# Values and seven heads' gates by seven products of quarters in a stage ahead of the heads, with token sums in SBUF, and two products of the output projection sharing a quarter of the weight

## The chip, the cores and the metric

The kernel runs on one core of one Trainium2 chip. The time is device microseconds (us) of one execution, as the median of several runs. The profile is of one such execution. The engines are TensorE (PE, matmuls; PEld are its weight loads), VectorE (DVE), ScalarE (ACT), GpSimd (POOL) and SyncE (SP, which issues most transfers here). Tensors lie in DRAM, in SBUF (128 partitions) or in PSUM, where the PE writes its sums. "128x1024" is a tile of 128 partitions with 1024 elements each.

## The reference

The function is a backbone of two layers over 256 latent tokens and 256 context tokens, in float32, with a width D of 2048. Each layer normalises its input, scales and shifts it by vectors computed from a condition (`mod = silu(c) @ ada_w + ada_b`, one for latents, one for context), runs a mixer with a SiLU gate, and adds the gated result. Layer 0 is retention with 8 heads (queries and keys 256 wide, values and gates 512 wide each); layer 1 is attention. Cut to what the change touches:

```python
def project(h):                                   # h: tokens x 2048
    p = h @ w_in                                  # w_in: 2048 x 12288
    q = heads(p[..., :2048], 8, 256) * 256 ** -0.5
    k = heads(p[..., 2048:4096], 8, 256)
    v = heads(p[..., 4096:8192], 8, 512)
    g = p[..., 8192:]                             # 8 heads x 512
...
o = retention of (q, k, v), both directions       # decays 2 ** (lg2 * distance)
on = o * rsqrt(mean(o * o) + EPS) * norm_gain
y = (on * silu(g)) @ w_out                        # 4096 x 2048
x = x + gate_latent * y_latent; ctx = ctx + gate_context * y_context
```

## The kernel before, in words

**Split precision.** Each float32 operand is held as a high part (rounded, `fp32r` in the profile) and a low part (the rest). A product is three matmuls, high·high, high·low and low·high (`mm3`, lines 140 to 142); in later stages the low part of the tokens and the high part share one 512-wide matmul, and the third is 256 wide (lines 188 and 191, 986 and 989). A weight tile `wraw` is 128x1024, 512 KB; SP loads it (`load_raw`, three buffers), ACT casts the high part `wh` (line 132), DVE subtracts to get the low part `wl` (`sub`, line 113), and 24 matmuls of 512 columns use the pair.

**Stages.** (1) Normalisation, the first modulation vectors, and the queries and keys of heads 0 and 1. (2) The heads: for each head a product for the gate, one for queries and keys and one for the values (`gemm_ws`, `gemm_ts`), each of eight weight tiles. Between the tiles a `hook` runs: one step of `sum_jobs`, two steps of `ada_jobs`, and one task of the list `tasks` (`pump`), which holds the work of the head before: scores, outputs, norm, `spill` and `parts`. (3) The output projection by seven products of quarters, M1 to M7 (a scheme of Strassen's kind: sums and differences of quarters of the tokens and of the weight are multiplied, so that eight products become seven). (4) Layer 1: keys, values, gates, queries, attention, its output projection.

**Side work in the heads stage.** `ada_jobs` computes the remaining modulation vectors on DVE: it loads rows of `adaB` into `abraw` tiles (128x512), and a SCALAR_TENSOR_TENSOR with an accumulated sum (line 711) multiplies each with the condition's row `crow`, once for each of two conditions, and writes the product to `ajunk`. `sum_jobs` makes four of the projection's weight sums in DRAM (`wS_d`): ACT's queue copies one quarter there and POOL's queue adds another with an accumulating transfer; a one-column copy `pin_t` on POOL sets when it is issued. `decays` makes the table `dd` of a head with a power on POOL (line 776). `output` adds squares `ossq` on POOL (line 829) and multiplies by the gate `sg` on DVE (line 825), `parts` makes sums `ue` of quarters of the gated output, which go to `uB_d` in DRAM, on POOL (line 843). What one of these engines does is in the order in which the program issues it; a transfer starts when its buffer is free.

**M3 and M6** run one after the other: M3 with a quarter of `wo0`, M6 with `wS_d[1]`, each as `single`, which splits one tile for each step.

## Time and profile before

| what | value |
|---|---|
| time, median of three runs | 1963.08 us (1960.08 to 1963.69) |
| span of the profiled execution | 1959.6 us |
| instructions in the profile | 26859 |
| ACT cast `wh`, each | 1052 ns, 415 of them |
| bytes moved | 436.23 MB, mean 223 GB/s |
| PEclk | 9 tenths or more in every slice |

The profiled execution's own time is not given apart; its span is 3.5 us below the median of the runs. The profile divides the span in 40 equal slices of 49 us; a digit is the busy share of an engine in tenths. Slices 3 to 24 are the heads, to slice 32 the projection, the rest is layer 1. A row of a timeline has the start, the duration, engine, line, operation and tiles; "xN" gathers N neighbours, and a start-to-start distance is the cost of one in a busy queue, since neighbours overlap at their ends. A row of a group has the count, the busy time, the mean of one in ns, and behind the second bar the idle time before these instructions and what ended it.

### The profile page before, as it was taken

How to read it: one execution, taken by the hardware profiler on the slowest of the kernel's cores; microseconds unless marked ns; L12 is line 12 of the kernel's file. 1: busy time of each engine (PE TensorE's matmuls, PEld its weight loads, DVE VectorE, ACT ScalarE, POOL GpSimd, SP SyncE). 2: the span in 40 equal slices, each digit the busy share in tenths (PEclk: the TensorE clock that was granted, in tenths of full speed). 3: DMA queues.
4: the chain of work that ended last, by engine and by line, in shares of the span. 5: the costliest groups of instructions: out<-in, count | busy, mean ns of one | idle time of the engine just before them, and what ended most of it. 6: DMA issues, size and time to landing. Idle time of an engine off the chain costs nothing.

```text
span 1959.6 us, 26859 instructions
## 1 busy us (share of the span) xinstructions
PE 1945.1 (99%) x9612; PEld 1612.6 (82%) x9612; DVE 1350.5 (69%) x2518; ACT 752.2 (38%) x1126; POOL 481.6 (25%) x389
## 2 busy tenths in 40 slices
PE   8999999999999999999999999999999999999999
PEld 4678888888888888888888888888888888888887
DVE  5566223788888888888565645877879746777764
ACT  4234223132222232232232334455555434766653
POOL 1218635525525526526300301100000100000000
PEclk9999999999999999999999999999999999999999
DMA  9965668898898998998755445677876324433365
GB/s 392 410 221 165 195 179 232 253 317 253 261 309 251 268 309 242 275 301 242 231 190 198 145 136 174 223 242 269 276 244 216 109 90 162 146 135 139 130 204 172
DMA packets 152039, 436.23 MB, mean 223 GB/s; under 512 B 18240, under 2 KB 37024, under 8 KB 146272
## 3 DMA queue, kind: packets, MB, share of 16 engines
q1 hardware_dynamic: 118976, 346.88, 50.6%
q0 software_dynamic: 10640, 34.87, 10.0%
q10 hardware_dynamic: 22288, 52.75, 7.8%
q8 instruction: 75, 1.23, 0.2%
q14 instruction: 60, 0.49, 0.1%
HBM read 416.04 MB, written 85.51 MB: 256 GB/s over the span
## 4 chain that ended last, share of the span: by engine, by line
PE 97%; DMA 1%; DVE 1%; issue 0%; ACT 0%; SPq 0%; DVEq 0%; ACTq 0%
PE acc L140 19%; PE acc L141 19%; PE acc L142 19%; PE acc L989 9%; PE acc L191 6%; PE acc L986 5%; PE acc L188 3%; PE pm L140 3%; PE pm L141 3%; PE pm L142 3%; PE acc L513 2%; PE pm L989 2%; PE pm L450 1%; PE pm L986 1%; PE pm L1307 1%; DMA rows<-gamT_d 1%
## 5 line engine op out<-in xcount | busy, mean ns | idle before, releaser
L132 ACT CAST wh<-wraw 128x1024 fp32r<-128x1024 f32 x415 | 435.2, 1052 | 848.5 <-PE acc L141 305.7
L113 DVE TENSOR_TENSOR wl<-wraw,wh 128x1024 fp32r<-128x1024 f32 x416 | 512.1, 1235 | 338.1 <-ACT wh L132 303.8
L140 PE MATMUL acc<-hT_h,wh 128*128 128x512 f32 x928 | 363.2, 391 | 1.0 <-DVE r_l L113 1.0
L141 PE MATMUL acc<-hl,wh 128*128 128x512 f32 x928 | 361.4, 389 | 0.0
L142 PE MATMUL acc<-hT_h,wl 128*128 128x512 f32 x928 | 361.2, 389 | 0.0
L711 DVE SCALAR_TENSOR_TENSOR ajunk<-abraw,crow 128x512 bf16<-128x512 f32 x448 | 344.2, 768 | 21.0 <-DMA abraw<-in_adaB 11.7
L142 PE MATMUL acc<-wh,hl 128*128 128x512 f32 x704 | 274.4, 390 | 0.0
L140 PE MATMUL acc<-wh,hT_h 128*128 128x512 f32 x576 | 224.7, 390 | 0.0
L141 PE MATMUL acc<-wl,hT_h 128*128 128x512 f32 x576 | 224.4, 390 | 0.0
L140 PEld LDWEIGHTS acc<-hT_h,wh 128*128 128x128 f32 x928 | 174.3, 188 | 38.0 <-DVE r_l L113 1.4
L142 PEld LDWEIGHTS acc<-hT_h,wl 128*128 128x128 f32 x928 | 174.2, 188 | 36.4
L141 PEld LDWEIGHTS acc<-hl,wh 128*128 128x128 f32 x928 | 174.4, 188 | 34.8
L241 POOL TENSOR_TENSOR rs<-ms,mhalf 128x4 f32<-128x4 f32 (+1 forms) x23 | 32.7, 1420 | 605.1 <-DVE ms L238 303.1
L776 POOL TENSOR_TENSOR dd<-two,dd 128x128 f32<-128x128 f32 x8 | 168.5, 21064 | 19.1 <-DVE dd L774 19.1
L142 PEld LDWEIGHTS acc<-wh,hl 128*128 128x128 f32 x704 | 132.2, 188 | 27.5
L322 POOL COPY pin_t<-wl 128x1 f32<-128x1 f32 x128 | 64.1, 500 | 317.5 <-DVE wl L113 313.2
L140 PEld LDWEIGHTS acc<-wh,hT_h 128*128 128x128 f32 x576 | 108.2, 188 | 23.1 <-issue 1.1
L141 PEld LDWEIGHTS acc<-wl,hT_h 128*128 128x128 f32 x576 | 108.2, 188 | 21.7
L324 POOL DMA_DIRECT2D wS_d<-in_wo x128 | 109.6, 872 | 11.2 <-issue 10.0
L843 POOL TENSOR_TENSOR ue<-sg 128x512 f32<-128x512 f32 x38 | 66.8, 1770 | 100.5 <-DVE sg L833 40.2
L829 POOL TENSOR_TENSOR ossq<-ossq,osq 128x512 f32<-128x512 f32 x24 | 35.3, 1470 | 185.7 <-ACT osq L823 185.0
L140 PE MATMUL acc<-wh,hl 128*128 128x512 f32 x192 | 75.4, 393 | 0.0
(282 smaller groups left out, 2915.1 us busy)
## 6 DMA issues: line engine op xcount, KB each, us to landing
wraw<-in_w SPq DMA_DIRECT2D x272, 512.0 KB, 4.2
abraw<-in_adaB SPq DMA_DIRECT2D x256, 256.0 KB, 5.5
wraw<-in_wo SPq DMA_DIRECT2D x80, 512.0 KB, 4.2
wS_d<-in_wo ACTq DMA_DIRECT2D x128, 256.0 KB, 5.2
wS_d<-in_wo POOLq DMA_DIRECT2D x128, 256.0 KB, 6.7
wraw<-wS_d SPq DMA_DIRECT2D x64, 512.0 KB, 4.5
araw<-in_adaS SPq DMA_DIRECT2D x28, 1024.0 KB, 11.5
wraw<-uB_d SPq DMA_DIRECT2D x20, 512.0 KB, 4.4
```

Source lines behind the costliest of these rows:

```text
L113: return nc.vector.tensor_tensor(out=out, in0=a, in1=hi.bitcast(F32), op=ALU.subtract)
L132: last_hi[0] = nc.scalar.copy(wh, raw).ins
L140: nc.tensor.matmul(ps, lhsT=ah, rhs=bh, start=start, stop=False, skip_group_check=skip)
L141: nc.tensor.matmul(ps, lhsT=ah, rhs=bl, start=False, stop=False, skip_group_check=skip)
L142: return nc.tensor.matmul(ps, lhsT=al, rhs=bh, start=False, stop=stop, skip_group_check=skip).ins
L191: nc.tensor.matmul(accs[j], lhsT=wk, rhs=h1(kb, s).rearrange("p a t -> p (a t)"), start=(kb == 0), stop=False)
L324: nc.gpsimd.dma_start(out=wS_d[i, r, q, x], in_=wo0_d[(*SUMS[i][1], r, q, x)], accum_op=ALU.add, max_dma_last_dim=4096)
L711: nc.vector.scalar_tensor_tensor(out=junk, in0=raw, scalar=1.0, in1=crow[:, t, q * 512:(q + 1) * 512], op0=ALU.mult, op1=ALU.mult, accum_o ...
L776: nc.gpsimd.tensor_tensor(out=dd, in0=two.to_broadcast([P, P]), in1=dd, op=ALU.pow)
L843: (nc.vector if now else nc.gpsimd).tensor_tensor(out=ue, in0=x, in1=y, op=op)
L986: last_pe[0] = nc.tensor.matmul(accs[j][:, 0:L], lhsT=wk, rhs=b[:, 0:L], start=False, stop=(kq == 3 and k == 3)).ins
L989: nc.tensor.matmul(accs[j], lhsT=wk, rhs=b, start=(kq == 0 and k == 0), stop=False)
```

## The change

Line numbers move: the subtraction of line 113 is line 114 after, that of a general sum or difference (`comb`) line 117, the ada operation of line 711 line 684, 829 and 843 are 1060 and 1074.

- **A new stage ahead of the heads.** The queries and keys of heads 0 to 2 go to DRAM (`stash`, `qk_d`). In the product of head 2's, `stat_jobs` makes four sums of quarters of the tokens and splits them into the SBUF tiles `S` (16 sums on DVE, 16 on POOL, 128x512 each). Then come four units for the values, each of two heads, and seven for the gates of heads 0 to 6. A unit is seven products of quarters: 28 steps for a pair of values, 14 for a gate. Step i loads its raw tile, forms the weight's sum or difference for step i-1 (`form`, 128x1024, on POOL but for half of `Y2`), splits that of step i-2 and multiplies that of i-3. `join` adds products on DVE from PSUM and an SBUF tile, and results go to `v_d` and `g_d` in DRAM; a gate's halves are added on POOL first.
- **Side work there.** After each step but those of the third product an ada step runs in two of three, and a sum job in one of four.
- **The ada operations** are 1024 wide, one for each condition, half as many. Their raw tiles are `wraw` tiles, of which there are now five. The last of their four parts moves to layer 1, where every second hook has one.
- **The heads** have six hooks each: five products for queries and keys and one for a gate are left, and the tasks stand in `slots` at numbered hooks. Queries and keys, values and gates come from DRAM. `dd` is read from a table in DRAM.
- **M3 and M6** are one stage. POOL adds the first quarter to the second for M6, and the sum jobs make three sums instead of four.

In instructions: matmuls of 512 columns 7275 to 6187, of 256 columns 1696 to 3152; casts of `wh` on ACT 416 to 506; POOL operations on two tiles of 128x1024 none to 121; ada operations on DVE 448 of 128x512 to 224 of 128x1024.

On POOL in the heads stage, before: at the end of a head the sums of squares and the `ue` of `parts`, 512 columns wide, with the copies and transfers of the weight sums.

```order
L829 TENSOR_TENSOR ossq<-ossq,osq 128x512 x2
L241 TENSOR_TENSOR rs<-ms,mhalf 128x4
L322 COPY pin_t<-wl 128x1
L324 DMA wS_d<-in_wo 64x1024
L843 TENSOR_TENSOR ue<-sg 128x512 x2
```

After, on POOL in a unit of values (lines 760, 762, 764 and 767 are `form`; `vt` is the formed tile):

```order
L760 TENSOR_TENSOR vt<-wraw 128x1024 x2
L326 COPY pin_t<-wl 128x1
L328 DMA wS_d<-in_wo 64x1024
L760 TENSOR_TENSOR vt<-wraw 128x1024 x2
L326 COPY pin_t<-wl 128x1
L328 DMA wS_d<-in_wo 64x1024
L762 TENSOR_TENSOR vt<-wraw,vt 128x1024 x3
```

POOL has a two-tile operation of 1024 columns at every second step; before, its two-tile operations were 512 wide and eight of them came with a head. On POOL in a unit of gates, after (line 862 adds the halves of a result):

```order
L862 TENSOR_TENSOR f<-f 128x2x256
L760 TENSOR_TENSOR vt<-wraw 128x1024
L862 TENSOR_TENSOR e<-e 128x2x256
L760 TENSOR_TENSOR vt<-wraw 128x1024
L326 COPY pin_t<-wl 128x1
L328 DMA wS_d<-in_wo 64x1024
L862 TENSOR_TENSOR f<-f 128x2x256
L762 TENSOR_TENSOR vt<-wraw,vt 128x1024
```

There the adds of results stand between the forms. On DVE in the heads stage, before: one low half and four ada operations for each weight tile.

```order
L113 TENSOR_TENSOR wl<-wraw,wh 128x1024
L711 SCALAR_TENSOR_TENSOR ajunk,asum<-abraw,crow 128x512 x4
L833 SCALAR_TENSOR_TENSOR sg<-sg,vec,pm 128x512 x4
L113 TENSOR_TENSOR wl<-wraw,wh 128x1024
L711 SCALAR_TENSOR_TENSOR ajunk,asum<-abraw,crow 128x512 x4
```

After, on DVE in a unit of values: a low half at each step, for 12 matmuls, an ada operation at two of three, and the joins (`q_1766` is a partial result).

```order
L114 TENSOR_TENSOR wl<-wraw,wh 128x1024
L684 SCALAR_TENSOR_TENSOR wraw,asum<-wraw,crow 128x1024
L114 TENSOR_TENSOR wl<-vt,wh 128x1024
L114 TENSOR_TENSOR wl<-wraw,wh 128x1024
L684 SCALAR_TENSOR_TENSOR ajunk,asum<-wraw,crow 128x1024
L117 TENSOR_TENSOR q_1766<-pm,q_1766 128x512
L114 TENSOR_TENSOR wl<-vt,wh 128x1024
L117 TENSOR_TENSOR q_1766<-pm,q_1766 128x512
L684 SCALAR_TENSOR_TENSOR wraw,asum<-wraw,crow 128x1024
```

The low halves come twice as often for a matmul as before. The diff, cut to its core:

```diff
-ADAN = (2, 2, 2)
+ORDER4 = ("X0 Z0 X1 Z1 X2 Z2 X3 Z3", "Y0 Z0 Y1 Z1 Y2 Z2 Z3 Y3", "Y0 Y1 Y2 Y3", "X0 Y0 X1 Y1 X2 Y2 X3 Y3")
+ORDER2 = ("X0 Z0 X1 Z1", "Y0 Z0 Z1 Y1", "Y0 Y1", "X0 Y0 X1 Y1")
...
     def load_raw(src):
-        t = strm.tile([P, 2, 512], F32, name="wraw", tag="wraw", bufs=3)
+        t = strm.tile([P, 2, 512], F32, name="wraw", tag="wraw", bufs=5)
...
     def sum_jobs():
-        todo = [(i, r, q, slice(64 * x, 64 * x + 64)) for i in (2, 3, 0, 1) for r in range(4) for q in range(4)
+        todo = [(i, r, q, slice(64 * x, 64 * x + 64)) for i in (2, 3, 0) for r in range(4) for q in range(4)
...
+                for kb in range(KB):
+                    raw = load_raw(adaB_d[16 * part + kb, q].rearrange("p (a c) -> p a c", a=2))
+                    for t in range(ntk):
+                        flat = raw.rearrange("p a c -> p (a c)")
+                        junk = pool.tile([P, 1024], BF16, name="ajunk", tag="ajunk") if t < ntk - 1 else flat
+                        nc.vector.scalar_tensor_tensor(
+                            out=junk, in0=flat, scalar=1.0, in1=crow[t],
+                            op0=ALU.mult, op1=ALU.mult, accum_out=asum[:, q, kb, t:t + 1])
+                        if (kb, t) != (KB - 1, ntk - 1):
+                            yield
+                if q:
...
+        def stat_jobs():
...
+
+            for kp in range(4):
+                ra, rb = t2(0), t2(1)
+                r = [ra[:, 0], ra[:, 1], rb[:, 0], rb[:, 1]]
+                for j, x in enumerate(r):
+                    k, c = 2 * kp + 8 * (j % 2), half(j // 2)
+                    nc.vector.tensor_tensor(out=x, in0=hT_h[:, k:k + 2, c].bitcast(F32),
+                                            in1=hl[k // 2][:, :, c].bitcast(F32), op=ALU.add)
+                a11, a12, a21, a22 = r
+                for out, x, y, op in ((a22, a21, a22, ALU.add), (a21, a11, a21, ALU.subtract),
+                                      (a11, a22, a11, ALU.subtract), (a12, a12, a11, ALU.subtract)):
+                    nc.gpsimd.tensor_tensor(out=out, in0=x, in1=y, op=op)
+                yield
+                ks = slice(2 * kp, 2 * kp + 2)
+                for i, x in enumerate((a22, a11, a21, a12)):
+                    split(S[i][:, ks, 0, :], S[i][:, ks, 1, :], x)
+                yield
+
...
+            def load(self, g, m, kp):
+                for b in {"X0": (11,), "Z0": (11, 12), "Y1": (22,), "Z1": (22,), "Y2": (11,), "X3": (21,),
+                          "Y3": (21,)}[f"{m}{g}"]:
+                    if (g, b, kp) not in self.raws:
+                        self.raws[g, b, kp] = load_raw(self.piece(b, kp))
+
+            def form(self, g, m, kp):
+                raws, vt = self.raws, self.vt
+                pool = nc.gpsimd.tensor_tensor
+                if (g, m) == (0, "Z"):
+                    vt[kp] = ph.tile([P, 2, 512], F32, name="vt", tag=f"T{kp if self.n == 4 else kp + 2 * (self.h % 2)}")
+                    pool(out=vt[kp], in0=raws[0, 12, kp], in1=raws[0, 11, kp], op=ALU.subtract)
+                elif (g, m) == (1, "Y"):
+                    pool(out=vt[kp], in0=raws[1, 22, kp], in1=vt[kp], op=ALU.subtract)
+                elif (g, m) == (2, "Y"):
+                    (pool if kp % 2 else nc.vector.tensor_tensor)(
+                        out=raws[2, 11, kp], in0=vt[kp], in1=raws[2, 11, kp], op=ALU.subtract)
+                elif (g, m) == (3, "Y"):
+                    pool(out=vt[kp], in0=raws[3, 21, kp], in1=vt[kp], op=ALU.subtract)
+
+            def parted(self, g, m, kp):
+                src = {"X0": 11, "Z1": 22, "X3": 21, "Y2": 11}.get(f"{m}{g}")
+                self.sp[g, m, kp] = split_w(self.raws[g, src, kp] if src else self.vt[kp])
...
+                else:
+                    wh, wl = (x.rearrange("p a (k c) -> p (a k) c", k=2) for x in (wh, wl))
+                    for t in range(2):
+                        ts = slice(t * P, t * P + P)
+                        for k4 in range(4):
+                            first, end = new and (kp, k4) == (0, 0), last and k4 == 3
+                            mh, ml = op(4 * kp + k4)
+                            if i is not None:
+                                nc.tensor.matmul(acc[t], lhsT=wh[:, k4, ts],
+                                                 rhs=S[i][:, 4 * kp + k4].rearrange("p a t -> p (a t)"),
+                                                 start=first, stop=end, skip_group_check=True)
+                            else:
+                                nc.tensor.matmul(acc[t][:, 0:L], lhsT=wh[:, k4, ts], rhs=mh, start=first, stop=False,
+                                                 skip_group_check=True)
+                                nc.tensor.matmul(acc[t][:, L:T], lhsT=wh[:, k4, ts], rhs=ml, start=False, stop=end,
+                                                 skip_group_check=True)
+                        for k4 in range(4):
+                            mh, ml = op(4 * kp + k4)
+                            nc.tensor.matmul(acc[t][:, 0:L], lhsT=wl[:, k4, ts], rhs=mh, start=False,
...
+                wide_hook(g)
+                if last:
+                    self.join(g, m)
...
+            def join(self, g, m):
...
+                if (g, m) == (0, "X"):
+                    self.q1 = self.tile("q1")
+                    each(lambda t, a: nc.scalar.copy(self.q1[:, t], a))
+                elif (g, m) == (0, "Z"):
+                    self.e = self.tile("e")
...
+                    each(lambda t, a: comb(self.f[:, t], a, self.q1[:, t], ALU.add))
+                elif (g, m) == (1, "Y"):
+                    each(lambda t, a: comb(self.f[:, t], a, self.f[:, t], ALU.add))
+                    self.store(0, 1, self.f)
+                elif (g, m) == (3, "X"):
+                    x = self.tile("f")
...
+            def store(self, i, j, t):
+                def finish():
+                    if self.kind == "v":
+                        nc.scalar.dma_start(out=v_d[self.h + j, :, 2 * i:2 * i + 2], in_=t)
+                    else:
+                        nc.scalar.activation(t[:, :, 0:L], t[:, :, 0:L], AF.Silu)
+                        nc.scalar.dma_start(out=g_d[self.h, :, 2 * j:2 * j + 2, half(i)], in_=t[:, :, 0:L])
+
+                if self.kind == "g":
+                    nc.gpsimd.tensor_tensor(out=t[:, :, 0:L], in0=t[:, :, 0:L], in1=t[:, :, L:T], op=ALU.add)
+                later.append((step_n[0] + (3 if self.kind == "g" else 1), finish))
+
+        def wide_hook(g):
+            step_n[0] += 1
+            n = step_n[0]
+            if g != 2 and n % 3:
+                ada_step()
+            if n % 4 == 0:
+                next(sums, None)
+            while later and later[0][0] <= n:
+                with tc.issue_after(last_hi[0]):
+                    later.pop(0)[1]()
+
...
+        def hook():
+            with tc.issue_after(last_lo[0]), tc.issue_after(last_hi[0]):
+                next(stats, None)
+            ada_step()
...
+        stash(2, gemm_ws(w0_d, 6, 8, h_mov, T, hook=hook))
+        us = [Unit("v", h) for h in (0, 2, 4, 6)] + [Unit("g", h) for h in range(H - 1)]
+        steps = [(u, g, x[0], int(x[1])) for u in us for g, xs in enumerate(ORDER4 if u.n == 4 else ORDER2)
+                 for x in xs.split()]
+        for i in range(len(steps) + 3):
+            for what, back in (("load", 0), ("form", 1), ("parted", 2), ("mm", 3)):
+                if 0 <= i - back < len(steps):
+                    u, *a = steps[i - back]
+                    getattr(u, what)(*a)
+        for _, f in later:
+            f()
...
-            nc.gpsimd.tensor_tensor(out=dd, in0=two.to_broadcast([P, P]), in1=dd, op=ALU.pow)
+            nc.scalar.dma_start(out=dd, in_=skew_d[h, 127:127 + P * 254].rearrange("(p x) -> p x", x=254)[:, 0:P])
             return rows, dd
...
+                    (nc.scalar if h == H - 1 else nc.gpsimd).dma_start(out=uB_d[m, h], in_=ue)
             for m, x in ((M2, a), (M5, d)):
...
+                at(b + 1 - i, lambda h=h, i=i: v_load(h, i))
+            for i in range(4):
+                at(b + (0 if late else 2 + i // 2), lambda h=h, i=i: scores(h, 0, (2, 3, 0, 1)[i], *rd[h]))
...
+        def hook():
+            next_slot()
+            n = state["n"]
+            next(sums, None)
+            ada_step(2 if n % 4 else 1)
...
+        def weights36(r, kq):
+            a, b = quarter(wo0_d[0, 0], r, kq), quarter(wo0_d[1, 0], r, kq)
+            yield split_w(a)
+            nc.gpsimd.tensor_tensor(out=b, in0=b, in1=a, op=ALU.add)
+            yield split_w(b)
...
+    def hook1():
+        pump(PUMP)
+        ada1_n[0] += 1
+        if ada1_n[0] % 2:
+            ada1_hook()
```

More of the change, by code (lines that the diff above doesn't have):

```diff
@@ L739, in qk_evac, with grid, v_load @@
+        def grid(x):
+            return x.rearrange("p (r c) -> p r c", r=4)
+        def v_load(h, i):
+            raw = load_raw(v_d[h, :, 2 * i:2 * i + 2])
+            for t in range(2):
+                split(slot_h(4 + 2 * i + t)[:, :], slot_l(4 + 2 * i + t)[:, :], raw[:, t])
+        state = {"n": 0}
         def qk_evac(ps, i, base):
@@ L1034, in stage @@
                     hook(r, kq)
+                    next(sums, None)
         def single(m, src, done, hook):
@@ L1342, in backbone @@
                     attend(c, t)
+        for _ in ada1:
+            pass
         for g in range(4):
```

417 lines of the change are left out of this document (252 added, 165 removed).

## The prediction

> **What bounds the kernel now.** I read the page first: busy time, slices, chain.
>
> ```profile
> PE 1945.1 (99%) x9612; PEld 1612.6 (82%) x9612; DVE 1350.5 (69%) x2518; ACT 752.2 (38%) x1126; POOL 481.6 (25%) x389
> PE   8999999999999999999999999999999999999999
> ...
> DVE  5566223788888888888565645877879746777764
> ...
> POOL 1218635525525526526300301100000100000000
> PE 97%; DMA 1%; DVE 1%; issue 0%; ACT 0%; SPq 0%; DVEq 0%; ACTq 0%
> ```
>
> TensorE is busy 99% of the span and is 97% of the chain: a matmul removed is time removed, as long as VectorE (DVE), which makes the low half `wl` of every weight tile, keeps up. DVE runs at 8 tenths in the heads stage (slices 8 to 18). So I looked at one head (heads are periodic; 400 to 544.9 us is one), at the products M3 and M6 (1405 to 1493 us) and at layer 1, by a table of stretches (busy time and count of PE, weight loads, DVE, ACT, POOL, then clock, DMA share, GB/s), and at DVE's groups in that head:
>
> ```profile
> 400.00:544.90 144.90, 144.90 (x662) 120.48 (x661) 122.44 (x277) 39.91 (x57) 66.39 (x58) 1.00 0.90 279
> 1405.00:1493.00 88.00, 88.00 (x508) 77.29 (x507) 70.96 (x111) 47.12 (x72) 1.49 (x1) 1.00 0.72 244
> 1640.00:1880.00 240.00, 239.99 (x1265) 202.76 (x1264) 183.59 (x320) 153.93 (x266) 9.29 (x8) 1.00 0.43 145
> L711 DVE SCALAR_TENSOR_TENSOR ajunk<-abraw,crow 128x512 bf16<-128x512 f32 x99 | 74.8, 756 | 5.9 <-DMA abraw<-in_adaB 3.7
> L113 DVE TENSOR_TENSOR wl<-wraw,wh 128x1024 fp32r<-128x1024 f32 x24 | 30.4, 1266 | 7.9 <-ACT wh L132 3.6 <-POOL pin_t L322 2.0 <-DMA wraw<-in_w 1.4
> ```
>
> DVE is at 122.44 of 144.90 us; less `ajunk` and `wl`, some 17.5 us of it are the head's own work. The granted clock is 1.00, and transfers run to 279 GB/s with the PE still full.
>
> **Price of a matmul.** From the timeline of PE, starts of single ones in the heads, and of runs of eight near the end:
>
> ```profile
> 376.10 0.39 PE L141 MATMUL acc<-hl,wh 128*128 128x512 f32 x1
> 376.33 0.39 PE L142 MATMUL acc<-hT_h,wl 128*128 128x512 f32 x1
> ...
> 1902.12 2.00 PE L191 MATMUL acc<-hT_h,wh 128*128 128x512 f32 x8
> 1903.96 1.11 PE L188 MATMUL acc<-hT_h,wl 128*128 128x256 f32 x8
> 1904.92 0.86 PE L191 MATMUL acc<-hT_h,wh 128*128 128x512 f32 x3
> ```
>
> (1903.96−1902.12)/8 = 0.230 us for 512 columns, (1904.92−1903.96)/8 = 0.120 for 256.
>
> **Price of POOL beside DVE.** The change gives POOL operations on two SBUF tiles, 1024 wide. The widest of before are 512 wide (`ue`, `ossq`). The timelines of DVE and POOL around two pairs of them:
>
> ```profile
> 374.60 1.22 DVE L113 TENSOR_TENSOR wl<-wraw,wh 128x1024 fp32r<-128x1024 f32 x1
> 375.74 1.78 DVE L711 SCALAR_TENSOR_TENSOR ajunk<-abraw,crow 128x512 bf16<-128x512 f32 x1
> ...
> 379.26 0.69 DVE L711 SCALAR_TENSOR_TENSOR ajunk<-abraw,crow 128x512 bf16<-128x512 f32 x1
> ...
> 380.00 0.69 DVE L711 SCALAR_TENSOR_TENSOR ajunk<-abraw,crow 128x512 bf16<-128x512 f32 x1
> ...
> 380.62 2.34 DVE L113 TENSOR_TENSOR wl<-wraw,wh 128x1024 fp32r<-128x1024 f32 x1
> 374.78 3.89 POOL L843 TENSOR_TENSOR ue<-sg 128x512 f32<-128x512 f32 x2 [5.32 <-DVE sg L833]
> 380.58 3.52 POOL L843 TENSOR_TENSOR ue<-sg 128x512 f32<-128x512 f32 x2 [0.61 <-DMA uB_d<-ue]
> 358.93 0.69 DVE L825 TENSOR_TENSOR sg<-pm,sg 128x512 f32<-128x512 f32 x1
> 359.54 1.42 DVE L711 SCALAR_TENSOR_TENSOR ajunk<-abraw,crow 128x512 bf16<-128x512 f32 x1
> 358.84 3.25 POOL L829 TENSOR_TENSOR ossq<-ossq,osq 128x512 f32<-128x512 f32 x2
> L829 POOL TENSOR_TENSOR ossq<-ossq,osq x24: 1280/1537/1717, 255.2 to 1186.8; 128x512 f32<-128x512 f32 x24
> L1365 POOL TENSOR_TENSOR xo<-xo,half x12: 732/738/745, 1887.4 to 1935.8; 128x256 f32<-128x256 f32 x12
> ```
>
> The same `ajunk` takes 0.69 us alone and 1.78 beside POOL, `wl` 1.22 and 2.34: +1.09 and +1.12, with one POOL operation in each. The two engines go one after the other. `sg<-pm,sg`, one of whose inputs is in PSUM, keeps its 0.69 in the middle of POOL's `ossq`. So a POOL operation of 512 columns takes about 1.06 us (these two and a shorter one) from a DVE that reads two SBUF tiles, of its own shortest 1.280. From 738 ns (256 columns) to 1280 (512) POOL needs 542 per 256, so 1024 columns take 1.280+2×0.542 = 2.36 us; less the same 0.22 that did not hold DVE, 2.14. That is my price of a hold. The bounds: 1.06 if a hold doesn't grow with width, 2×1.28 = 2.56 if two whole short ones.
>
> The Trainium skill (SBUF — State Buffer, "Who interferes with whom") states that a DVE instruction with two SBUF inputs contends with a GpSimd one that reads SBUF, and that the first to issue keeps the shared ports for the whole instruction. The rows above agree at 512 columns; no row shows 1024. By that rule the hold is the 2.14 and the sum below +63; by the nearest row alone, 1.06, it is −42.
>
> DVE, start to start: `wl` 375.74−374.60 = 1.14; `ajunk` 0.74 and 0.62 (379.26, 380.00, 380.62), mean 0.68 with its accumulator read; a 512-wide operation of 0.69 about 0.61. For the 1024-wide `ajunk`:
>
> ```profile
> L113 DVE TENSOR_TENSOR wl<-wraw,wh 128x1024 fp32r<-128x1024 f32 x416 | 512.1, 1235 | 338.1 <-ACT wh L132 303.8
> L113 DVE TENSOR_TENSOR r_l<-acc,r_h 128x512 fp32r<-128x512 f32 x36 | 24.0, 686 | 6.0 <-ACT r_h L116 5.8
> L776 POOL TENSOR_TENSOR dd<-two,dd 128x128 f32<-128x128 f32 x8 | 168.5, 21064 | 19.1 <-DVE dd L774 19.1
> ```
>
> 1235−686 = 0.55 us for 512 columns more, so 0.68+0.55 = 1.23.
>
> **The parts and the sum**, against the span of 1959.6 us.
>
> *TensorE.* Values go from 8×8×24 = 1536 to 4×28×12 = 1344 matmuls of 512, seven gates from 1344 of 512 to 448 of 512 and 1456 of 256. Saved: 1088×0.230 = 250.2; added: 1456×0.120 = 174.7. Net **−75.5 us**, if the PE is fed.
>
> *Values units* (4 of 28 steps). PE: 112×12×0.230 = 309. DVE: 112 `wl` ×1.14 = 127.7; two ada steps in three outside the third product, 64×1.23 = 78.7; 40 joins ×0.61 = 24.4; 8 of the `Y2` forms, 9.1; together 240. POOL: 14 forms each, 56×2.14 = 120. As DVE and POOL go in turn, 360 against 309: +51. Joins read PSUM and can run under a hold; POOL holds a third of the time, so a third of 24.4 comes off: **+43**.
>
> *Gate units* (7 of 14 steps). PE: 56 steps of 8×0.230+8×0.120 = 2.80 and 42 of 24×0.120 = 2.88: 278. DVE: 98×1.14 = 111.7, 56×1.23 = 68.9, 70 joins 42.7, 7 forms 8; 231. POOL: 49×2.14 = 104.9 and 28 adds of 2x256 ×1.06 = 29.7; 135. 366−278 = +88, less joins under the hold, 135/366 of 42.7 = 16: **+72**.
>
> *Token sums* in the queries-and-keys product of head 2. DVE: 8 `wl`, 16 adds and 16 low halves at 0.61, seven `ajunk`: 9.1+19.5+8.6 = 37; POOL 16×1.06 = 17: 54 against 8×24×0.230 = 44: **+10**.
>
> *Heads stage*, now 48 hooks. PE: 48×24×0.227 = 262 and the heads' own matmuls, (144.90−24×24×0.227)×8 = 113; some 375. DVE: 8×17.5 = 140, 48×1.14 = 55, 64×1.23 = 79; with 64 holds of 1.06 (`ue`, `ossq`) 341, 91%. Before it was 122.44+8×1.06 = 131 of 144.90, also 90%, with a full PE. I take **+5** for places where a head's work is denser than the mean; ends 0 and +40.
>
> *M3 with M6.* DVE keeps its 70.96 us of the 88, and 16 sums of quarters on POOL hold it 34: 105. Some of DVE's work there reads PSUM, and residuals can run late: half, **+8**; ends 0 and +24 (16×2.56+71−88).
>
> *Layer 1* gets 32 `ajunk`, 39 us of DVE in a stage with 56 idle in 240: 0. That cover holds only if the idle time is spread; it was at every second hook.
>
> *At nothing:* POOL's `dd`, 168.5 us, was on no wait of the PE (1% of the chain is DVE, POOL doesn't appear in it); DMAs on POOL's queue (`ue` to DRAM) stand behind forms, and what reads them is a stage away. The transfers, by the rates of the queues:
>
> ```profile
> q1 hardware_dynamic: 118976, 346.88, 50.6%
> q0 software_dynamic: 10640, 34.87, 10.0%
> ```
>
> 346.88 MB in 50.6% of 1959.6 us is 350 GB/s at full share, 34.87 in 10.0% 178 (these are nearly all accumulating ones). A values unit has 20 weight tiles and 8 ada tiles of 512 KB, 7 sums of two times 256 KB and 2 MB of results: 18.6 MB/350+1.8/178 = 63 us of 77. The heads stage has 48 weight tiles, 35 ada tiles, 40 sums, 23 MB of reloaded values, gates, queries and keys, and some 23 MB more to and from DRAM: 99.6/350+10.5/178 = 344 of 375 us, 0.92, beside 0.90 in the head of before. So loads cost nothing where they come early. A form waits for its raw tile; behind it on POOL stand the next form and the sums' `pin_t` copies, which nobody needs soon. A late form makes the next `wl` late, and the load that waits for the buffer: the bound counted above, not another. On ACT a gate's Silu waits for POOL's add; it is issued three steps later, so that the casts behind it find it done.
>
> −75.5+43+72+10+5+8 = +62.5: span 2022, and as the median of the runs (1963.08) stands 3.5 above the profiled span, **2025 us**.
>
> **The rivals.**
> *Hold doesn't grow, or is covered (faster).* One mechanism: a 1024-wide POOL operation takes from DVE no more than a 512-wide one. At 1.06 the values need 240+59 = 299 of 309 (0), the gates +19, M3 with M6 0, token sums and heads +15: −75.5+34 = −42, 1921 us. For: no row shows a 1024-wide hold. Against: the time of POOL grows straight with width. It decides at a hold h with 113h = 179, 1.58 us.
> *Partly covered:* DVE often waits for ACT's `wh` (303.8 us over the run), and a hold could fall there. With a fifth to a third of the 225 us of long holds outside DVE's work 45 to 75 us come off: 1950 to 1980 us. Against: those idle times come from a DVE that is ahead; a late one has none.
> *Heads stage late too:* the denser hooks (a value split, two `ajunk`, eight rotations) put +40 there instead of +5: 2060 us. Holds of 2.56 alone give 105×0.42 = +44 in both units, 2069; both together 2104.
> *Transfers bind:* at 0.92 of their time in the heads stage they would, if bunched; it has the same place and price as the rival before and goes with it.
>
> **How the numbers follow.** Another run tells apart 0.2%, 4 us. Chances: as worked, 1990 to 2060, 0.50; heads late as well or holds longer, 2060 to 2095, 0.15; partly covered, 1950 to 1990, 0.15 (0.03 faster, 0.03 the same, 0.09 slower); not binding, 1890 to 1950, 0.17; above 2095, 0.03. Faster 0.20, same 0.03, slower 0.77. The range of 1950 to 2095 leaves out 0.20; the likeliest case's own is 1990 to 2060.
>
> **What would show it.** In the profile after: PE below 9 tenths in the new stage, with its idle time ended by `wl`; POOL's `vt` at 2.4 us or longer; `wl` beside it lengthened by about 2.1; DVE and POOL together filling the stage; joins of unchanged length; some 90 us a values unit, 52 a gate unit. It is wrong if PE stays at 9 throughout that stage, if `wl` grows by 1 us only, or if time goes in the heads stage or on loads.

## The result, and the profile after

The changed kernel takes 2174.45 us (median of 4, 2169.13 to 2175.51) where the kernel before takes 1963.15: a ratio of 1.1074, 95% interval 1.1058 to 1.1089. It is slower, as forecast, but by 211 us and not by 62, and outside the range. The profiled execution's span is 2173.7 us, 214.1 more than before.

The page of the changed kernel, the lines that answer to those of before:

```profile
PE 1967.0 (90%) x9980; PEld 1628.7 (75%) x9980; DVE 1735.2 (80%) x2297; ACT 899.7 (41%) x1308; POOL 739.7 (34%) x514
PE   8988798888888888888998989999998899999999
...
DVE  4648979798899999977787878677788974888965
...
POOL 0114446545566766632444443510014210000001
PEclk9999999999999999989999999999999999999999
```

PE is busy for 90% of the span instead of 99%, and 22 us longer although it has less to do. By stage (busy times as in the prediction's tables; the last three columns are PEclk, the transfers' share and GB/s), after: the product with the token sums, values, gates, heads, M4 to M2, M3 with M6, layer 1.

```profile
147.90:217.60 69.70, 55.40 (x206) 41.44 (x205) 50.99 (x60) 21.49 (x30) 30.84 (x19) 0.91 0.50 164
217.60:592.80 375.20, 324.89 (x1334) 258.18 (x1333) 327.15 (x282) 124.79 (x127) 192.83 (x105) 0.94 0.69 219
592.80:947.50 354.70, 302.99 (x1906) 272.38 (x1905) 332.19 (x287) 131.99 (x152) 230.78 (x126) 0.94 0.68 205
947.50:1394.90 447.40, 398.11 (x1824) 327.66 (x1824) 343.27 (x609) 172.41 (x318) 175.49 (x182) 0.94 0.81 260
1394.90:1626.00 231.10, 227.14 (x1283) 198.97 (x1282) 181.82 (x232) 120.75 (x168) 25.19 (x19) 0.99 0.81 259
1626.00:1740.90 114.90, 97.18 (x522) 83.99 (x521) 101.85 (x124) 48.17 (x72) 39.91 (x15) 0.91 0.47 153
1740.90:2173.70 432.80, 422.80 (x2174) 355.71 (x2172) 317.20 (x528) 229.87 (x364) 27.83 (x37) 1.00 0.56 181
```

Before, the same places (heads, M4 to M2, M3 and M6, layer 1):

```profile
147.90:1219.80 1071.90, 1070.92 (x4898) 891.26 (x4897) 728.28 (x1519) 307.41 (x442) 424.13 (x336) 1.00 0.76 233
1219.80:1443.80 224.00, 224.00 (x1281) 196.34 (x1280) 178.04 (x226) 119.92 (x167) 6.00 (x3) 1.00 0.75 253
1443.80:1534.20 90.40, 90.40 (x522) 79.34 (x520) 78.04 (x131) 48.88 (x74) 1.49 (x1) 1.00 0.57 195
1534.20:1959.60 425.40, 421.14 (x2175) 355.83 (x2173) 280.44 (x453) 223.47 (x358) 27.89 (x37) 1.00 0.43 144
```

Two things are new. PE idles (a stretch less its PE busy time), and PEclk is below 1: the record of the granted clock has 32 places between 148 us and the last microseconds with half the clock, each 3.41 us or a multiple of it, 181 us in all; before, none there. What they follow, on the PE's timeline in the heads stage:

```profile
1017.15 0.40 PE L146 MATMUL acc<-hT_h,wl 128*128 128x512 f32 x1
1017.38 0.95 PE L253 MATMUL pm<-ones,ossq 128*128 128x1 f32 x8
1024.48 1.11 PE L259 MATMUL pm<-ident,rs 128*128 128x128 f32 x4 [6.16 <-POOL rs L245]
1025.25 0.78 PE L144 MATMUL pm<-r_h 128*128 128x512 f32 x1
1025.82 0.63 PE L145 MATMUL pm<-r_l,r_h 128*128 128x512 f32 x1
1026.25 0.63 PE L146 MATMUL pm<-r_h,r_l 128*128 128x512 f32 x1
1026.67 0.63 PE L144 MATMUL pm<-r_h 128*128 128x512 f32 x1
1027.10 0.51 PE L145 MATMUL pm<-r_l,r_h 128*128 128x512 f32 x1
```

After a wait of 6.16 us the same matmul starts every 0.43 us (1025.82, 1026.25, 1026.67, 1027.10) instead of 0.23: nearly half of the time is lost. The record has half the clock here from 1020.52 to 1027.35, so it begins while PE still waits; of the 181 us at half clock, PE is busy for 141. So the time of a stage is its work at full clock, its idle time, and about half of the time that PE is busy at half clock:

| stage | took | idle | PE busy at half clock | idle + half of that | forecast |
|---|---|---|---|---|---|
| token sums' product | 69.7 | 14.3 | 12.4 | 21 | 10 |
| values | 375.2 | 50.3 | 30.9 | 66 | 43 |
| gates | 354.7 | 51.7 | 37.1 | 70 | 72 |
| heads | 447.4 | 49.3 | 41.6 | 70 | 5 |
| M4 to M2 | 231.1 | 4.0 | 6.2 | 7 | 0 |
| M3 with M6 | 114.9 | 17.7 | 12.8 | 24 | 8 |
| layer 1 (more than before) | 432.8 | 5.7 | 0 | 6 | 0 |
| sum | | 193 | 141 | 264 | 138 |

What is left without both columns agrees with kernels that wait far less: 224 us for M4 to M2 and 91 for M3 with M6 (before: 224.0 and 90.4), 309 for the values (306 and 309 in two versions below). 214 − 264 leaves −50 us of work saved, where −75.5 was forecast. Of the 25 us between, some 15 are in neither column: an idle time is counted from the modelled end of the last matmul, 0.40 us after its start, where a busy queue would start the next after 0.23, and there are 88 such waits ahead of layer 1. Some 3 are the price, 0.227 us from start to start in the heads of before where the sum took 0.230; the rest was not located. The table doesn't say that the clock is 70 us of the loss: where VectorE sets the pace a slow PE only waits less.

What PE waited for, in us, times and the longest, in the values and then in the gates:

```profile
PE acc L145 <- DVE wl L114: 24.7, 13, 5.9
PE pm L145 <- DVE wl L114: 13.8, 6, 4.5
```

```profile
PE pm L804 <- DVE f L117: 24.0, 9, 5.8
PE pm L814 <- DVE wl L114: 16.2, 7, 4.1
```

Both are DVE's: the low halves, as foreseen, and in the gates even more the joins (`f`).

The hold at 1024 columns, on the timeline of DVE in a values unit:

```profile
310.54 1.22 DVE L114 TENSOR_TENSOR wl<-wraw,wh 128x1024 fp32r<-128x1024 f32 x1
311.68 3.42 DVE L114 TENSOR_TENSOR wl<-vt,wh 128x1024 fp32r<-128x1024 f32 x1
```

POOL's timeline at the same place:

```profile
311.32 2.70 POOL L760 TENSOR_TENSOR vt<-wraw 128x1024 f32<-128x1024 f32 x1 [1.69 <-DMA wraw<-in_w]
```

And of the tile `vt` the forms of one line, with their shortest, median and longest in ns:

```profile
L767 POOL TENSOR_TENSOR vt<-wraw,vt x30: 2359/2776/3441, 272.0 to 926.9; 128x1024 f32<-128x1024 f32 x30
```

3.42 against 1.22: 2.20 us (2.14 estimated), and the shortest form takes 2.36 (2.36 estimated). So the hold grows with the operation. This agrees with the Trainium skill (SBUF — State Buffer, "Who interferes with whom"), by which the ports that DVE and GpSimd share are an exclusive lock; that the first to issue keeps them for the whole instruction it says of DVE's two-port modes, and here it is seen with two SBUF inputs. The joins, which read PSUM, kept their length (0.68 us each). But not all of a form's time was taken from DVE. DVE's low halves in the values, in the changed kernel and then in the version with the forms on DVE (below):

```profile
L114 DVE TENSOR_TENSOR wl<-wraw,wh 128x1024 fp32r<-128x1024 f32 x63 | 120.2, 1911 | 13.0 <-ACT wh L136 12.1 <-issue 0.4
L114 DVE TENSOR_TENSOR wl<-wraw,wh 128x1024 fp32r<-128x1024 f32 x64 | 77.9, 1218 | 6.6 <-ACT wh L136 6.6
```

By such differences over all of DVE's 1024-wide operations, POOL took 96 us from DVE in the values and 105 in the gates, where the sum, with the joins taken off, had 112 and 119. DVE was busy for 327 of 375 us and 332 of 355: nearly full, not filled.

### The profile page after: what moved, and what is told of

Its sections match the earlier page's. It is cut to its first block, busy times and chain, and to the rows that moved or that the text cites. A ratio compares the mean times of both kernels' runs of the same rounds, so it can differ in the third digit from the quotient of the medians.

```text
span 2173.7 us, 27677 instructions
## 1 busy us (share of the span) xinstructions
PE 1967.0 (90%) x9980; PEld 1628.7 (75%) x9980; DVE 1735.2 (80%) x2297; ACT 899.7 (41%) x1308; POOL 739.7 (34%) x514
## 5 line engine op out<-in xcount | busy, mean ns | idle before, releaser
L144 PE MATMUL acc<-hT_h,wh 128*128 128x512 f32 x480 | 193.6, 403 | 10.9 <-ACT wh L136 10.0
L146 PE MATMUL acc<-hT_h,wl 128*128 128x512 f32 x480 | 190.9, 403 | 11.0 <-DVE wl L114 10.9
L145 PE MATMUL acc<-hl,wh 128*128 128x512 f32 x480 | 191.7, 399 | 0.0
L684 DVE SCALAR_TENSOR_TENSOR wraw<-wraw,crow 128x1024 f32<-128x1024 f32 x128 | 190.0, 1485 | 0.0
L114 DVE TENSOR_TENSOR wl<-vt,wh 128x1024 fp32r<-128x1024 f32 x90 | 169.4, 1883 | 24.3 <-ACT wh L136 24.1
L136 ACT CAST wh<-vt 128x1024 fp32r<-128x1024 f32 x90 | 94.7, 1052 | 200.0 <-PE pm L804 54.3
L684 DVE SCALAR_TENSOR_TENSOR ajunk<-wraw,crow 128x1024 bf16<-128x1024 f32 x96 | 144.3, 1503 | 28.4 <-DMA wraw<-in_adaB 28.4
L146 PE MATMUL acc<-wh,hl 128*128 128x512 f32 x320 | 125.9, 393 | 0.0
L760 POOL TENSOR_TENSOR vt<-wraw 128x1024 f32<-128x1024 f32 x30 | 86.1, 2869 | 85.1 <-DMA wraw<-in_w 64.6
L762 POOL TENSOR_TENSOR vt<-wraw,vt 128x1024 f32<-128x1024 f32 x30 | 84.5, 2838 | 35.7 <-DMA wraw<-in_w 19.8
L767 POOL TENSOR_TENSOR vt<-wraw,vt 128x1024 f32<-128x1024 f32 x30 | 85.4, 2889 | 27.0 <-DMA wraw<-in_w 25.8
```

What stands on the lines that cost most here:

```text
L114: return nc.vector.tensor_tensor(out=out, in0=a, in1=hi.bitcast(F32), op=ALU.subtract)
L136: last_hi[0] = nc.scalar.copy(wh, raw).ins
L144: nc.tensor.matmul(ps, lhsT=ah, rhs=bh, start=start, stop=False, skip_group_check=skip)
L145: nc.tensor.matmul(ps, lhsT=ah, rhs=bl, start=False, stop=False, skip_group_check=skip)
L146: return nc.tensor.matmul(ps, lhsT=al, rhs=bh, start=False, stop=stop, skip_group_check=skip).ins
L684: nc.vector.scalar_tensor_tensor(out=junk, in0=flat, scalar=1.0, in1=crow[t], op0=ALU.mult, op1=ALU.mult, accum_out=asum[:, q, kb, t:t + 1])
```

## The experiments

The theory: the units and M3 with M6 are late by POOL's hold on DVE; the PE's waits then halve its clock. Rivals: transfers and buffers; DVE alone; in the heads stage also the order of small operations. A version that was run once is compared with the changed kernel's 2174 us and its stage times. Stages that an edit leaves alone scatter: the changed kernel and three versions that don't touch the heads stage took 447 to 456 us there.

**Forms on DVE.**

```diff
-                pool = nc.gpsimd.tensor_tensor
+                pool = nc.vector.tensor_tensor
```

> All 105 long forms of weights (v and g units) on VectorE instead of 98 on GpSimd; M3 with M6 unchanged. Port theory (a two-tile GpSimd operation holds VectorE for about 2.1 us at 1024 columns, the same form costs VectorE 1.14 itself): the values part falls from 378 us to 310-335, the gates part from 352 to 305-330, the whole from 2174 to 2070-2100; the time at half clock in these two parts falls from 85 to under 30 us. Rival, transfers (five raw buffers and the order of loads pace the steps): both parts within 10 us of now. Rival, VectorE alone is the bound and the port is free: 105 x 1.14 us more work, slower by 60-110.

Measured: 2089.95 us. Values and gates:

```profile
216.50:539.40 322.90, 311.19 (x1334) 252.19 (x1333) 297.58 (x342) 125.14 (x127) 38.53 (x50) 0.98 0.81 255
539.40:858.30 318.90, 293.30 (x1906) 263.57 (x1905) 307.32 (x333) 129.27 (x150) 93.28 (x76) 0.98 0.75 227
```

322.9 and 318.9 us, half clock 24 us instead of 85. DVE does 98 operations more and is busy for less: what POOL took from it was worth more than the operations. The port theory holds, its rivals fall. The form also takes 1.22 us on DVE instead of 2.4 or more on POOL, so this edit alone doesn't part the hold from a late form.

**Ada operations of 8 columns in the units** (`thin` sets the width; the same in the heads next).

```diff
-                            out=junk, in0=flat, scalar=1.0, in1=crow[t],
+                            out=junk[:, n], in0=flat[:, n], scalar=1.0, in1=crow[t][:, n],
```

> Leaves out work: the ada operations in the units read 8 of their 1024 columns, so the later modulation vectors are not those of the reference; loads, order and counts stay. Port theory: VectorE has 120 x 1.15 = 138 us less to do, values 312-325 us (PE 309), gates 290-305 (PE 278), whole 2060-2085. Transfers theory: both parts within 10 us of 378 and 352, since every load stays.

Measured: 2132.86 us, values 350.8, gates 328.6. A miss: 138 us of DVE's work out brought 50, with 33 and 35 us of idle left, though DVE, with the time for which it was held, was busy for only 232 and 248 us there. POOL's form is also a link in each step's chain (raw tile, form, cast, low half), 2.4 to 3.5 us long; DVE now waited 107 us for casts in the two parts. Moving the form shortens both; less other work only one.

**The same in the heads.**

> Leaves out work: the ada operations in the heads stage read 8 of 1024 columns, nothing else changes. If the heads stage (448 us where its matmuls need 375) is late because VectorE and GpSimd are too dense there, 70 x 1.15 = 80 us less of VectorE bring it to 385-405 us and its half-clock time from 55 to under 20. If it is late because the norm's small operations stand behind other work of the next head in the queues of VectorE and ScalarE (order, not load), it falls by less than 25 us and the waits of the transposes for rs stay at 10 us or more.

Measured: 2159.51 us; heads 423.5 (24 less), idle 32.5, half clock 34, waits for `rs` 8.0. It lies between the two expectations: DVE's load is a part, not the whole.

**M6's sum on DVE.**

```diff
-            nc.gpsimd.tensor_tensor(out=b, in0=b, in1=a, op=ALU.add)
+            nc.vector.tensor_tensor(out=b, in0=b, in1=a, op=ALU.add)
```

> The 16 sums of quarters for M6 on VectorE instead of GpSimd. Port theory: VectorE needs 71 + 16 x 1.14 = 89 us instead of 71 + 16 x 2.2 = 106, the joint stage falls from 115 us to 92-102. Rival, the stage is late by the chain load, sum, cast, low half for each tile: also shorter, since a sum takes 1.2 instead of 2.75 us, but it stays above 105. Rival, the residual's work makes it late (waits for x): unchanged at 112-118.

Measured: 2155.00 us; the joint stage:

```profile
1623.80:1718.00 94.20, 92.50 (x522) 80.70 (x521) 88.30 (x137) 48.27 (x72) 1.58 (x1) 0.98 0.56 182
```

94.2 instead of 114.9, in the port theory's range. All but 4 us of that stage's loss was POOL's part in it.

**Waits put into the kernel before**, to price the clock where nothing else is late.

```diff
-        nc.gpsimd.tensor_tensor(out=rs, in0=ms, in1=mhalf.to_broadcast([P, n]), op=ALU.pow)
+        for _ in range(1 + again[0]):
+            nc.gpsimd.tensor_tensor(out=rs, in0=ms, in1=mhalf.to_broadcast([P, n]), op=ALU.pow)
```

> The kernel before, with the power for rs repeated 3, 4, 4, 5, 5, 6, 7 times more in heads 0 to 6 (same result): by 1.45 us a repeat and 3.1 us of slack the PE waits some 1.2, 2.7, 2.7, 4.2, 4.2, 5.6, 7.0 us, 28 in all, at the transposes. Clock theory (a wait of some 2.5 us or more is followed by 3.4 to 6.8 us at half clock): six windows and 10 to 20 us of lost work on top, the whole slower by 36 to 50 us. Rival (the lower clock is a record without effect, or the work queued behind runs faster for it): slower by the waits alone, 25 to 31 us.

Measured: 1986.22 us, ratio 1.0129 (1.0114 to 1.0144), +25 us. The waits were shorter than expected, 1.7, 1.7, 2.8, 2.8, 3.5, 4.6 and none in the seventh head. The stretch that took 1071.9 us before:

```profile
147.90:1244.80 1096.90, 1079.71 (x4901) 895.66 (x4900) 729.32 (x1521) 308.43 (x443) 459.75 (x370) 0.99 0.75 228
```

On PE's timeline a wait with what follows it:

```profile
969.03 0.65 PE L258 MATMUL pm<-ident,rs 128*128 128x128 f32 x4 [3.49 <-POOL rs L244]
...
970.67 0.63 PE L140 MATMUL acc<-hT_h,wh 128*128 128x512 f32 x1
971.10 0.63 PE L141 MATMUL acc<-hl,wh 128*128 128x512 f32 x1
```

16.2 us more idle, and one window of 3.4 us at half clock behind each of the four longer waits, 6.8 us of work: 23 of the 25. The two waits of 1.7 us brought none. The 36 to 50 us forecast were missed, since the waits were shorter, and 25 is a time that the rival had named; but with 16.2 us of waits the rival would have 16, so it falls. A half-clock window costs some 1.7 us where PE is the bound.

**The waits filled with spare matmuls.**

```diff
+                    for _ in range(FILL.get(h, 0)):
+                        nc.tensor.matmul(bp, lhsT=hT_h[:, 0, 0:P], rhs=hT_h[:, 0, :], start=True, stop=True)
                     st["bp"] = rstd_rows(st["rs"], bp, 0, 4)
```

> The same waits, but 5 to 30 spare matmuls of 512 columns (0.23 us each, their result is overwritten) stand ahead of the transposes and fill most of each wait. Clock theory: no half-clock time in the heads, slower than before by the waits alone, 25 to 32 us, and 10 to 20 us faster than the same waits left idle, though TensorE does 114 matmuls more. Rival: the same time as the unfilled one or slower.

> The kernel before with the same repeated powers, but with 6, 6, 11, 11, 14, 18 spare matmuls in heads 0 to 5: 15 us, fitted to the waits measured in the unfilled kernel (1.7, 1.7, 2.8, 2.8, 3.5, 4.6), where 117 of them were too many. Clock theory: no half-clock window; the part from 148 us to the projection takes 1087-1091 us, 6 to 10 less than the 1096.9 of the unfilled one, although TensorE does 66 matmuls more (before: 1071.9). Rival, the half clock costs nothing: 1096 or more.

Measured: 1987.91 us (1.0136, 1.0119 to 1.0153) and 1986.46 (1.0126, 1.0108 to 1.0144): no gain from either. With 117 spare matmuls there is no half clock in the heads; but 117×0.228 = 27 us is more than the waits were. The fitted 66 left one wait of 4.55 us behind its 18 spare ones, with 6.8 us of half clock, and the stretch took 1095.6 where 1087 to 1091 were expected. That a busy PE keeps its clock is shown; that filling pays is not.

**The norm's end one hook later**, and **a third `sw` buffer**, two guesses on the heads.

```diff
-            for i, f in zip((1, 2, 3, 4, 5) if late else (4, 5, 6, 7, 7) if p == 6 else (4, 5, 7, 8, 8), outs):
+            for i, f in zip((1, 2, 3, 4, 5) if late else (4, 5, 6, 7, 7) if p == 6 else (4, 5, 7, 9, 9), outs):
```

> The changed kernel with the two last tasks of a head (transposes of rs, spill, parts) one hook later. Order theory (the PE waits for a norm whose small operations stand behind the next head's work): the waits for rs, 14.6 us, vanish with some 8 us of half clock, the heads stage falls from 447 to 420-430 us. Density theory: the waits move to other places, 440 us or more.

> The changed kernel with three instead of two buffers for sw, for which ScalarE's copies wait in the rotation of queries and keys. If ScalarE, blocked behind such a copy, makes the heads stage late, that stage falls from 447 to 415-430 us; if the lateness is spread over many chains, it stays within 10 us.

Measured: 2180.49 and 2185.62 us; heads 457.5 and 447.5. What the PE waited for in the heads, in the changed kernel and then with the norm's end later:

```profile
PE pm L259 <- POOL rs L245: 14.6, 5, 6.2
PE pm L144 <- issue: 6.3, 1, 6.3
PE acc L146 <- DVE wl L114: 6.3, 3, 4.3
PE pm L253 <- POOL ossq L1060: 5.4, 2, 3.8
```

```profile
PE acc L146 <- DVE wl L114: 15.5, 8, 5.0
PE acc L144 <- ACT wh L136: 11.2, 3, 7.3
PE pm L253 <- POOL ossq L1060: 8.4, 3, 3.5
PE pm L144 <- issue: 6.5, 1, 6.5
PE pm L259 <- POOL rs L245: 3.8, 1, 3.8
```

The wait for `rs` fell from 14.6 to 3.8 us, and those for the weight tiles took its place: this order isn't the cause (others were not tried). Nor is ScalarE's wait for `sw`.

**The weight sums ahead of the heads.**

```diff
-            if n % 4 == 0:
+            if n % 2 == 0:
                 next(sums, None)
```

> The changed kernel with a sum job at every second step of the units, so that all 96 are done before the heads stage, which then has 21 MB less to transfer and 40 GpSimd copies and issues less. If transfers or GpSimd's queue make the heads stage late, it falls from 447 us to 400-425; else it stays within 10 us. The units: 44 jobs more, 0 to 10 us longer.

Measured: 2149.07 us. The heads:

```profile
961.50:1369.00 407.50, 385.95 (x1823) 319.55 (x1823) 343.76 (x608) 172.84 (x317) 122.50 (x104) 0.97 0.68 234
```

40 us less, the most of any edit to that stage alone, with DVE's busy time unchanged (343.76, 343.27). The transfers' busy time falls from 0.81×447.4 = 362 us to 0.68×407.5 = 277; 362 is 96% of the stage's 377 us of work. The units took 15 us longer (0 to 10 expected), so the whole gained 25.

**Bytes or queue?** Only 8 of 64 rows accumulated in the heads.

```diff
+                x = slice(x.start, x.start + few[0])
```

> Leaves out work: in the heads stage the accumulating transfers of the weight sums add 8 of their 64 rows, so three sums of the projection's weight are incomplete; every copy, issue and wait on GpSimd stays. 9.2 MB fewer at the 178 GB/s of that queue are 52 us less of the transfers' 363 us in that stage. If transfers make it late: 447 falls to 412-430 us. If GpSimd's queue does (its pin_t copies wait for VectorE, and ossq, rs and ue stand behind them): 440-455.

Measured: 2153.64 us; heads 424.9, transfers 0.75×424.9 = 319 us, POOL's work unchanged (174 us, was 175). Bytes alone make 22 of the 40 us; how the other 18 divide between the copies' bytes and the queues' entries was not tried.

**Plain gates, ahead of the heads.**

```diff
-        us = [Unit("v", h) for h in (0, 2, 4, 6)] + [Unit("g", h) for h in range(H - 1)]
+        us = [Unit("v", h) for h in (0, 2, 4, 6)]
...
+        for h in range(H - 1):
+            accs = gemm_ws(w0_d, 3 * h + 2, 8, h_mov, T, hook=hook_g)
```

> The changed kernel with plain products for the seven gates (8 tiles and 192 matmuls each, no forms, no joins), values still by seven products. PE needs 56 x 24 x 0.2275 = 306 us instead of 278, VectorE 56 x (1.14 + 1.23) = 133. Port theory: the gates part takes 306-312 instead of 355 us with under 3 us of idle and no half clock: 2120-2135 in all. Rival, a late start and end of each head's product cost it anyway: 330 or more.

Measured: 2133.87 us. Gates and heads together take 760.4 us instead of 802.1, with 50.5 of idle instead of 101: the gates' share of it is gone. (Some of the heads' scores ran among the gates, so the 306 alone can't be read off.) Seven products for the gates lose 42 us against plain ones.

**Plain gates among the heads**, forms and M6's sum on DVE, the gates of heads 1 to 6 between the products of the heads stage, slots spread over 88 hooks.

```diff
+            while state["n"] < 40 * n // 88:
+                next_slot()
...
+        plain_gate(1, hook)
         for h in range(3, H):
+            plain_gate(h - 1, hook)
```

> Values by seven products with all forms on VectorE, the M6 sum on VectorE, and plain gates: gate 0 ahead of the heads, the other six among the products of the heads stage, so that each head's scores, outputs and norm have 11 products' hooks instead of 5. Cover theory (the heads stage is late because each head's chain of small operations has 33 us of products to hide in, not 72): gates and heads together need 681 us of TensorE and take 685-705, with under 15 us of waits and under 10 us of half clock, instead of 802; the whole 1980-2005 us. Density theory (VectorE or transfers too full in the mean): over 730 us. Slower than the kernel before in any case by 1 to 2%, since the values part and the token sums still cost more than the 44 us of matmuls that they save.

Measured: 2002.55 us (1998.50 to 2005.69), ratio 1.0205 (1.0187 to 1.0223). Values, then gates and heads:

```profile
216.50:536.50 320.00, 308.93 (x1345) 251.20 (x1344) 298.34 (x345) 125.85 (x128) 37.29 (x52) 1.00 0.82 257
536.50:1239.10 702.60, 687.90 (x3157) 568.23 (x3157) 479.43 (x770) 245.71 (x399) 228.31 (x240) 0.99 0.80 262
```

Where the heads' work has twice the products to lie beside, the idle falls to 14.7 us, the half clock to 13.7. The same products also give the transfers more time, so this run doesn't part the two. It is the best of the changed versions, and not faster than the kernel before.

**A lighter start**, and **no ada in layer 1**, both on top of that.

```diff
-            if g != 2 and n % 3:
+            if g != 2 and n % 3 == 0:
...
-            ada_step(1 if n % 3 else 2)
+            ada_step(2)
```

> The version with the gates among the heads, and besides: the 16 token sums of GpSimd on VectorE with no ada operation beside them, one ada step in three in the values part and two at every hook of the heads, a sum job at every second step of the values. By the stage times so far: 148 to the sums, 50-56 for the sums' product (69 before), 310-315 for the values (320), 690-700 for gates and heads (703), 235 for M4 to M2, 94 for M3 and M6, 429 for the rest: 1956-1971 of span, 1960-1975 us, even with the kernel before or up to 0.7% slower. If the ada operations in the heads crowd VectorE (80% of that stage by count), the heads take 710 or more.

> The same with the fourth ada part in the heads stage too, instead of layer 1. If its 32 operations make layer 1 longer (429 us, before 421), that part falls to 420-423 us and the whole is 3-8 us faster than the version before it; if the heads cannot take them, VectorE at some 88% there, the heads get longer by 10 us or more.

Measured: 2047.04 us (1.0449, 1.0416 to 1.0482) and 2060.26 (1.0517, 1.0485 to 1.0548): worse, and the first forecast is missed by 70 us. The token sums' product did fall from 68.6 to 58.6 us, but values, gates and heads took 1076 instead of 1023: the values 30 us longer, gates and heads 23 (some 726, where 710 or more had been named for a crowded VectorE). With the fourth ada part there too, gates and heads took another 22. In the values, with twice the weight sums beside the values, though with half the ada operations, DVE waited for raw tiles:

```profile
DVE vt L768 <- DMA wraw<-in_w: 27.3, 10, 5.4
DVE vt L770 <- DMA wraw<-in_w: 14.0, 6, 5.7
DVE wraw L772 <- DMA wraw<-in_w: 13.9, 11, 2.5
DVE vt L775 <- DMA wraw<-in_w: 9.9, 5, 3.5
```

65 us, where the version before it waited 11 for the same tiles. Layer 1, from its first matmul to the end, took 426.2 us without its ada operations and 434.1 with (before: 425.1): its 8 us are theirs.

## Why the prediction was right or wrong

**Right: the sign, POOL's hold on DVE in the units, and its price.** POOL's two-tile operations hold DVE, 2.2 us at 1024 columns. Forms on DVE undo it in the values (323 us against 309 of work) and half of it in the gates (319 against 278), where the joins and POOL's adds are left. That the gates' +72 came out as 70 is luck in part. The sum gave them 350 us as DVE's work and POOL's hold, filled without a gap; DVE was busy for 332 and idle for 22. An eighth of the hold fell where DVE would have waited, as the rival "partly covered" had it, and waits that the sum didn't have took its place.

**Wrong: the heads, +5 forecast and 70 measured.** This step failed. It set DVE's 91% and the transfers' 0.92 beside the 90% and 0.90 of before and concluded that they cost nothing. The transfers' time there was 362 us, not 344, of 377 us of work; and each head's chains had 6 hooks to hide in instead of 24. Without the weight sums the stage is 40 us shorter (22 by their bytes alone), with less DVE work 24, with the norm's end later not at all, and with more products beside the heads nearly all of it goes: there is too little cover for transfers and DVE together. Which of the two is the larger is not shown. The rival "heads stage late too" had this as +40 and 0.15.

**Wrong: no term for the clock.** The sum let the PE catch up at full speed after each wait. PE was busy for 141 us at half clock. In the heads and in M3 with M6, where it adds to the waits, that costs 21 and 6 us; in the gates it stands within the 72 that were forecast.

**Mis-sized: smaller terms.** Values 66 for 43: DVE was idle there for 48 us, 20 of them until a cast and 16 until an ada tile had landed. A late form is also late in its chain, as the thin ada operations showed; its share was not measured apart from that of the transfers and of the clock (15 us at most). The matmuls saved 50 us by the table, 65 with the waits' uncounted ends, for 75.5. M3 with M6 24 for 8, its own upper end, where "half of it can run late" was a guess. The token sums' product 21 for 10. Layer 1 had "0, if the idle time is spread": 8 measured in one pair of versions. M4 to M2 had none: 7, with 4 us of idle in its first product.

**What stays open:** how far bytes and queue entries share the sums' last 18 us, and whether any version with seven products for the values gains: they save 192×0.230 = 44 us of matmuls by the prediction's price, and the best version tried is still 2% slower than the kernel before.

## What to carry to other kernels

Before work is moved to POOL to relieve DVE, add its duration to DVE's wherever both read two SBUF tiles, and compare the sum with the bound of that stage. When matmuls are taken out of a stage, the side work and transfers that they covered must be counted again per microsecond that is left, and 90% of three things at once is not a cover. In these kernels a PE that waited more than two or three microseconds at a time mostly paid again at half clock.

## What the runs showed of the hardware

Over 13 of these kernels (the changed one and its versions), a wait of PE that began at full clock was followed within 2 us by half clock in 41 of 261 cases when it was 1 to 2 us long, in 93 of 148 at 2 to 3 us, in 88 of 94 at 3 to 4 us, and in all 110 at 4 us or more.

What decides is where the wait lies. In each trace the half-clock windows start on one grid of 3.413 us. Over these 13 and the two kernels of before with half clock in the heads, from 150 us on, a full-clock window of this grid in which PE idled for more than 2 us (up to the modelled ends of its matmuls) was followed by half clock in all 269 cases, one with 1.8 to 2 us in 44 of 64, with 1.2 to 1.8 us in 26 of 263, with less in 1 of 7429. At half clock it takes less: 0.6 us of idle time in a window kept the half clock in 161 of 162 cases, less than that in 16 of 355. So a wait of 2.5 us can fall into two windows and bring no half clock, or into one and bring it.

The Trainium skill (TensorE: Matmul & The Clock Gate, "Part 1: The HAM clock gate") states half the clock after an idle window of about 3.4 us in a free-running count. The grid and the length of the windows agree; but the window need not be idle throughout, 2 us of it are enough here.
